# Convolution sums kept in two PSUM banks, with the weights' low parts and the running total made by GpSimd

## The chip, the cores and the metric

The kernel runs on one core of one Trainium2 chip. Its engines are TensorE (PE in the profile, with PEld for its weight loads), VectorE (DVE), ScalarE (ACT), GpSimd (POOL) and SyncE (SP, which here only issues DMAs). Each engine works through its own list of instructions in the order fixed when the program is built, and waits on semaphores for the others. The metric is the device time of one execution in microseconds, the median over runs. Before the change it is 1243.22 us (three runs, 1242.7 to 1243.86).

## The reference

One decoder layer on 1024 tokens of width 1024, float32. What matters here is the first half:

```
h = rmsnorm(x, norm_g) * (1 + scale) + shift
glu_a, glu_b, z_conv, q, k, v, z_att, g_conv, g_att = split(h @ w_in)
u = glu_a * sigmoid(glu_b)
u = causal depthwise convolution of u, 31 taps per channel, + conv_b
u = silu(layernorm(u, conv_ln_g, conv_ln_b))          # over the 1024 channels
y_conv = (u * silu(z_conv)) @ w_conv_out
... dilated attention of q, k, v gives y_att ...
merged = sigmoid(g_conv) * y_conv + sigmoid(g_att) * y_att
x = x + gate * (merged @ w_o);  out = rmsnorm(x, final_g)
```

The layer norm needs, for each token, the sum of the convolution's output over all channels, and then the sum of its squares.

## The kernel before

Channels lie on the 128 partitions and the 1024 tokens along the free dimension, so 1024 channels are eight tiles of 128 x 1024. To keep float32 precision at the speed of the matrix engine's fp32r type, every operand is split into a high part (rounded to fp32r, by ACT) and a low part (the rest, a subtraction). A product is then three matmuls: high by high, high by low, low by high (`mm3`, lines 72 to 75). `split` (line 55) makes both parts: line 57 is the ACT copy, line 58 the subtraction, on VectorE unless `lo_eng` names another engine.

An opening stage (to line 400) normalises x, makes the split input `hh`, `hl`, and computes the first projections. It uses a pool `pd` of eight PSUM banks of 128 x 512 float32. Its last matmuls are the first three projections (six banks called `first`) and, behind them, a row product (line 362) that ACT copies out at line 399.

The phase that the change touches is the loop at line 614 over the list `todo`. A `Unit` multiplies one column tile of 128 of `w_in` with the whole of h: two halves of 512 tokens, each 24 matmuls into one PSUM bank, which its `consume` then reads. A `Values` entry computes one group of the attention's v: eight tiles of 24 matmuls. `prepare` makes the split weights of the next entry while the present one runs: it loads a raw tile (three buffers, SP's queue) and splits it (two buffers each for high and low). For each of the eight channel tiles a `Glu` has two units: `sig` takes the sigmoid of `glu_b` on ACT (line 524), `glu` multiplies it with `glu_a` on VectorE (line 531) into a tile `u` of which there are two, whose 30 leading zeros GpSimd writes (line 529).

As soon as a `u` is complete, `conv` (line 437) is put into the list `behind`. It is a generator that issues the 31 taps on VectorE one at a time. Even taps are summed in `v` and odd taps in `v2`, so that neighbouring instructions do not depend on each other. The two are added (line 448), and `v` is added to the running total `tot1` over the channel tiles (lines 451, 454). A pump decides how these instructions are strewn among the matmuls: each quarter of a unit (12 matmuls) gives a credit of `PIECE` = 2.75, each tap takes `OP` = 1.25 of it, and other work on VectorE takes its share by `spend`. The build then orders each engine's instructions by this order of issue and by when they are ready.

When `todo` reaches entry `last_tap` (27), all taps left are issued (`drain`), and `norm` (line 567) takes their place in `behind`: the mean from a matmul of `ones` with `tot1` (line 572), its subtraction (578), squares on ACT and their total `tot2` (585), a matmul for the column sums (line 125), the reciprocal root, its row (line 140), scaling (597), gating (601) and the split of the result for the output projection, which begins at line 664. At line 680 `pd_ctx` is closed and the attention opens its own PSUM pools.

All PSUM pools are opened with `reuse_waits="tile"`: a tile of a new pool waits for the old tiles that lay in its place, not for the whole old pool. In the program before, other PSUM pools give their first tile their first bank.

Of the kernel before, what the change touches and what calls it, by code (L numbers as in the profile page):

```python
# [8 lines left out]
F32 = mybir.dt.float32  # L9
# [7 lines left out]
P = 128  # L17
S = 1024
D = 1024
KT = 8  # L20
TAPS = 31
# [18 lines left out]
def layer(ctx: ExitStack, tc: tile.TileContext, a, out):  # L40
    nc = tc.nc
    ctx.enter_context(nc.allow_non_contiguous_dma(reason="small gathers of row maxima"))
    add, mult, sub, mx = ALU.add, ALU.mult, ALU.subtract, ALU.max
# [5 lines left out]
    def psum_pool(name, **kw):  # L49
        return tc.tile_pool(name=name, space=PSUM, reuse_waits="tile", **kw)  # L50
# [4 lines left out]
    def split(hi, lo, raw, lo_eng=None):  # L55

        nc.scalar.activation(hi, raw, AF.Copy)  # L57
        (lo_eng or nc.vector).tensor_sub(lo, raw, hi.bitcast(F32))  # L58

    def load_raw(src, n=1024):  # L60
        raw = wpool.tile([P, n], F32, name="wraw", tag="wraw", bufs=3)
        nc.sync.dma_start(raw, src)
        return raw

    def weights(src, n=1024, lo_eng=None):
        raw = load_raw(src, n)
        hi = wpool.tile([P, n], F32R, name="whi", tag="whi")
        lo = wpool.tile([P, n], F32R, name="wlo", tag="wlo")
        split(hi, lo, raw, lo_eng)
        return hi, lo  # L70
# [20 lines left out]
    cw = taps.tile([P, KT, TAPS], F32, name="cw")  # L91
    cvec = taps.tile([P, 3, KT], F32, name="cvec")
# [23 lines left out]
    pd_ctx = ExitStack()  # L116
    pd = pd_ctx.enter_context(psum_pool("pd", bufs=8))
# [53 lines left out]
    with sbuf_pool("start") as st, tc.manual_schedule(  # L171
# [117 lines left out]
        for n, (x, c) in enumerate(zip((spread, cb[:, halves[1]]), halves)):  # L289
            nc.vector.tensor_tensor_reduce(out=wa_t[KT][:, c], in0=x, in1=wa_t[KT][:, c], scale=1.0, scalar=0.0,  # L290
                                           op0=mult, op1=add, accum_out=(gcol if n == 0 else scol)[:, 0:1])
# [115 lines left out]
    def slot(tag, name, dt=F32, bufs=1):  # L407
        return pb.tile([P, S], dt, name=name, tag=tag, bufs=bufs)

    def temp(name):  # L410
        return slot("tmp", name, bufs=3)
# [3 lines left out]
    PIECE, OP, HALF = 2.75, 1.25, 0.7  # L415
# [3 lines left out]
    def spend(us):  # L419
        credit[0] -= us  # L420

    def pump(us):
        credit[0] = min(credit[0] + us, 2 * PIECE)
        while credit[0] > 0 and behind:
            try:
                spend(next(behind[0]))
            except StopIteration:
                behind.pop(0)

    def drain():  # L430
        while behind:
            pump(2 * PIECE)

    tot1 = slot("l0", "tot1")
    v_t = [None] * KT

    def conv(ct, u):
        v = v_t[ct] = slot(f"v{ct}", f"v{ct}")
        v2 = temp("v2")
        nc.vector.tensor_scalar(v, u[:, 0:S], cw[:, ct, 0:1], cvec[:, 0, ct:ct + 1], op0=mult, op1=add)  # L440
        yield HALF
        nc.vector.tensor_scalar(v2, u[:, 1:1 + S], cw[:, ct, 1:2], None, op0=mult)
        yield HALF
        for k in range(2, TAPS):
            d = v2 if k % 2 else v
            nc.vector.scalar_tensor_tensor(d, u[:, k:k + S], cw[:, ct, k:k + 1], d, op0=mult, op1=add)  # L446
            yield OP
        nc.vector.tensor_add(v, v, v2)
        yield OP
        if ct == 0:  # L450
            nc.vector.tensor_copy(tot1, v)
            yield HALF
        else:
            nc.vector.tensor_add(tot1, tot1, v)
            yield OP

    def wide(half):
        return slice(half * 512, half * 512 + 512)

    class Unit:  # L460
# [3 lines left out]
            self.u, self.consume, self.cost = u, consume, cost  # L464

        def prepare(self):
            spend(OP)
            self.w = weights(a["w_t"][self.u])

        def run(self):  # L470
            hi, lo = self.w
# [12 lines left out]
    class Values:  # L484
# [5 lines left out]
        def prepare(self):  # L490
            self.w = []
            for kp in range(4):
                raw = load_raw(a["w_v"][self.g, kp])
                hi, lo = slot(f"z{kp}", f"vh{kp}", F32R), slot(f"z{4 + kp}", f"vl{kp}", F32R)
                split(hi, lo, raw)
                spend(OP)
                self.w.append((hi, lo))

        def run(self):
# [15 lines left out]
    class Glu:  # L515
# [10 lines left out]
        def glu(self, half, s, ps):  # L526
            if not half:
                self.u = up.tile([P, TAPS - 1 + S], F32, name="u", tag="u", bufs=2)
                nc.gpsimd.memset(self.u[:, 0:TAPS - 1], 0.0)
            o = TAPS - 1 + half * 512  # L530
            nc.vector.tensor_mul(self.u[:, o:o + 512], ps, self.sb[:, s])
            if half:
                behind.append(conv(self.ct, self.u))
# [33 lines left out]
    def norm():  # L567
        mean = up.tile([P, TAPS - 1 + S], F32, name="mean", tag="u", bufs=2)[:, 0:S]
        for half in range(2):
            s = wide(half)  # L570
            pm = bank()
            nc.tensor.matmul(pm, ones, tot1[:, s], start=True, stop=True)
            nc.scalar.activation(mean[:, s], pm, AF.Copy, scale=1.0 / D)
        yield 2 * PIECE
        lrow = up.tile([P, TAPS - 1 + S], F32, name="lrow", tag="u", bufs=2)[:, 0:S]
        tot2 = slot("l0", "tot2")
        for ct in range(KT):
            nc.vector.tensor_sub(v_t[ct], v_t[ct], mean)
            yield OP
            if ct == 0:  # L580
                nc.scalar.activation(tot2, v_t[ct], AF.Square)
            else:
                sq = temp("sq2")
                nc.scalar.activation(sq, v_t[ct], AF.Square)
                nc.vector.tensor_add(tot2, tot2, sq)
                yield OP
        yield PIECE
        pc = bank()[:, 0:8]
        col_sums(pc, tot2)
        lcols = rstd_cols(pc, "l")  # L590
        yield PIECE
        for half in range(2):
            half_row(lrow, lcols, half)
        yield PIECE
        for ct in range(KT):
            v = v_t[ct]
            nc.vector.tensor_mul(v, v, lrow)
            yield OP
            sg_ = temp("sgu")
            nc.scalar.activation(sg_, v, AF.Silu, scale=cvec[:, 1, ct:ct + 1], bias=cvec[:, 2, ct:ct + 1])  # L600
            nc.vector.tensor_mul(v, sg_, sz_t[ct])
            yield OP
            hi = slot(f"z{ct}", f"uh{ct}", F32R)
            lo = slot(f"v{ct - 1}" if ct else "l0", f"ul{ct}", F32R)
            split(hi, lo, v)
            yield OP
            ch[ct], cl[ct] = hi, lo
# [3 lines left out]
    for f, bb in ((g_.sig, first[0:2]), (g_.glu, first[2:4]), (second.sig, first[4:6])):  # L611
        for half in range(2):
            f(half, wide(half), bb[half])
    for n, unit in enumerate(todo):
        if n + 1 < len(todo):
            todo[n + 1].prepare()
        if n == last_tap:
            drain()
            behind.append(norm())
        for _ in unit.run():  # L620
            pump(PIECE)
# [65 lines left out]
    pd = c_ctx.enter_context(psum_pool("pd2", bufs=2))  # L687
# [140 lines left out]
    def pieces():  # L828

        for u in range(units):  # L830
            (hi, lo), consume = made_w.pop(u)
            for half in range(2):
                s = slice(half * 512, half * 512 + 512)
                ps = bank()
                for k in range(KT):
                    c = slice(k * P, (k + 1) * P)
                    mm3(ps, hi[:, c], lo[:, c], hh[:, k, s], hl[:, k, s], k == 0, k == KT - 1)
                    if k == 3:
                        yield None, (raw_for, u + 2) if half else (prepare, u + 1)
                yield lambda half=half, s=s, ps=ps: consume(half, s, ps), None  # L840

    k2, q2, v2 = {}, {}, {}
# [283 lines left out]
    for x, it in ((101, att_again(0)), (102, att_again(1)), (105, att_again(2)), (106, w_out(0, 0)), (109, w_out(0, 1)),  # L1126
                  (110, w_out(0, 2)), (111, first_ao())):
        in_steps(it, [x, x + 2])
    raw_for(0)
    prepare(0)  # L1130
    stream = pieces()

# [64 lines left out]
    pd = ctx.enter_context(psum_pool("pd3", bufs=8))  # L1197
# [12 lines left out]
    for d in range(KT):  # L1210
# [6 lines left out]
        hi, lo = hh[:, d, :], hl[:, d, :]  # L1217
# [127 lines left out]
```

## Time and profile before

| | |
|---|---|
| median of three runs | 1243.22 us |
| the profiled execution, first to last instruction | 1241.9 us |
| its granted TensorE clock, mean | 0.998 |
| PE busy | 1230.6 us, 6234 matmuls |
| VectorE busy | 909.5 us, 1500 instructions |
| ScalarE busy | 511.8 us, 1026 instructions |
| GpSimd busy | 91.1 us, 79 instructions |

The profile shows one execution; its time is the span from the first to the last instruction, and no other time of that execution is given. Groups of instructions are shown as: line, engine, operation, output tile <- input tiles, shapes, count, then total busy time in us and the mean of one in ns, then the engine's idle time just before them and what ended it. A timeline row has the start in us, the length in us, then the instruction; rows next to each other that are alike are merged with their count, and the length then covers all of them. A row of waits reads: who waited, for whom, the total in us, how often, the longest. Lengths of matmuls overlap, so the step from start to start tells PE's pace.

### The profile page before, as it was taken

What the parts mean: (1) busy time and instruction counts of PE and PEld (TensorE: products, weight loads), DVE (VectorE), ACT (ScalarE), POOL (GpSimd) and SP (SyncE); (2) the same over time, 40 slices, a digit from 0 to 9 for tenths busy, and PEclk for the clock granted to TensorE, in tenths of its full rate; (3) what the DMA queues carried; (4) which work ended last, traced back from release to release, by engine and by line L of the source; (5) the groups of instructions that cost most, each with busy time, mean ns of one, the idle gap of its engine ahead of it and who ended that gap; (6) DMA issues with size and microseconds to landing.
All of it is one profiled execution on the core that took longest, in us unless ns stands there. A gap on an engine that the chain in (4) does not pass through costs nothing.

```text
span 1241.9 us, 17026 instructions
## 1 busy us (share of the span) xinstructions
PE 1230.6 (99%) x6234; PEld 1033.2 (83%) x6234; DVE 909.5 (73%) x1500; ACT 511.8 (41%) x1026; POOL 91.1 (7%) x79
## 2 busy tenths in 40 slices
PE   9999999999999999999999999999999999999997
PEld 7787888888888888888888888888888888888886
DVE  7867999999999986873435657777786762449454
ACT  5653112111222235930114666666666665345211
POOL 0000000000000000000031111111111012100000
PEclk9999999999999999999999999999999999999999
DMA  9532311311211112355636555575666574668231
GB/s 358 195 106 72 114 52 50 110 60 51 86 54 49 51 55 80 127 172 203 191 74 165 128 139 145 157 186 145 161 187 151 138 183 130 207 232 297 87 102 68
DMA packets 89896, 165.09 MB, mean 133 GB/s; under 512 B 28563, under 2 KB 42195, under 8 KB 89814
## 3 DMA queue, kind: packets, MB, share of 16 engines
q1 hardware_dynamic: 73136, 157.40, 42.6%
q10 hardware_dynamic: 16678, 6.61, 2.0%
q8 instruction: 49, 0.80, 0.3%
q14 instruction: 33, 0.27, 0.1%
HBM read 105.48 MB, written 27.04 MB: 107 GB/s over the span
## 4 chain that ended last, share of the span: by engine, by line
PE 92%; DMA 3%; DVE 3%; ACT 1%; issue 1%; DVEq 0%; ACTq 0%; SPq 0%
PE d L73 22%; PE d L75 22%; PE d L74 22%; PE o L957 4%; PE s L920 3%; PE t L936 3%; PE d L1250 2%; PE d L1248 2%; PE d L506 2%; PE d L1249 2%; PE d L507 2%; PE d L505 2%; DMA sgr<-ascr 1%; DMA x<-in_xT 1%; PE d L271 1%
## 5 line engine op out<-in xcount | busy, mean ns | idle before, releaser
L73 PE MATMUL d<-hh,whi 128*128 128x512 f32 x1072 | 419.9, 392 | 0.0
L75 PE MATMUL d<-hh,wlo 128*128 128x512 f32 x1072 | 417.9, 390 | 0.0
L74 PE MATMUL d<-hl,whi 128*128 128x512 f32 x1072 | 417.9, 390 | 0.0
L446 DVE SCALAR_TENSOR_TENSOR v<-u,cw,v 128x1024 f32<-128x1024 f32 x232 | 280.3, 1275 | 0.0
L75 PEld LDWEIGHTS d<-hh,wlo 128*128 128x128 f32 x1072 | 201.3, 188 | 42.7
L73 PEld LDWEIGHTS d<-hh,whi 128*128 128x128 f32 x1072 | 201.4, 188 | 39.1 <-issue 0.2
L74 PEld LDWEIGHTS d<-hl,whi 128*128 128x128 f32 x1072 | 201.4, 188 | 38.7 <-issue 0.2
L57 ACT ACTIVATE whi<-wraw 128x512 fp32r<-128x512 f32 (+1 forms) x104 | 83.9, 827 | 212.3 <-PE d L74 203.1
L58 POOL TENSOR_TENSOR wlo<-wraw,whi 128x512 fp32r<-128x512 f32 (+1 forms) x56 | 81.7, 1476 | 636.0 <-ACT whi L57 624.2
L925 DVE CUSTOM_DVE_ANT_0 sb<-s,mask 128x128 f32<-128x128 f32 (+1 forms) x192 | 59.7, 348 | 53.6 <-PE s L920 52.3
L929 ACT ACTIVATE sb<-sb,stats 128x128 f32<-128x128 f32 (+1 forms) x192 | 84.8, 443 | 30.5 <-DVE stats L925 30.2
L936 PE MATMUL t<-ident,sb 128*128 128x128 f32 x280 | 73.7, 276 | 0.1
L957 PE MATMUL o<-ph,vt 128*64 128x128 f32 (+1 forms) x432 | 65.9, 253 | 0.0
L58 DVE TENSOR_TENSOR wlo<-wraw,whi 128x1024 fp32r<-128x1024 f32 (+1 forms) x48 | 54.8, 1141 | 14.6 <-ACT whi L57 14.1
L751 ACT ACTIVATE ph<-t 128x384 fp32r<-128x384 f32 (+2 forms) x96 | 45.8, 477 | 36.8 <-PE t L936 28.4
L754 DVE TENSOR_TENSOR pl<-t,ph 128x384 fp32r<-128x384 f32 (+2 forms) x96 | 52.0, 541 | 10.0 <-ACT ph L751 9.4
L920 PE MATMUL s<-k,ql 128*128 128x128 f32 (+1 forms) x192 | 55.0, 292 | 0.0
L957 PE MATMUL o<-pl,vt 128*64 128x128 f32 (+1 forms) x216 | 52.8, 261 | 0.0
L672 DVE TENSOR_TENSOR gs<-d,sgc 128x512 f32<-128x512 f32 x16 | 11.1, 691 | 54.9 <-PE d L75 48.6
L1250 PE MATMUL d<-oh,hl 128*128 128x512 f32 (+1 forms) x136 | 51.2, 376 | 0.0
L1248 PE MATMUL d<-oh,hh 128*128 128x512 f32 (+1 forms) x136 | 51.2, 376 | 0.0
L920 PE MATMUL s<-k,q 128*128 128x128 f32 (+1 forms) x192 | 51.1, 272 | 0.0
(242 smaller groups left out, 1917.0 us busy)
## 6 DMA issues: line engine op xcount, KB each, us to landing
wraw<-in_w_t SPq DMA_DIRECT2D x67, 512.0 KB, 4.2
k<-kqp SPq DMA_DIRECT2D x96, 128.0 KB, 2.3
q<-kqp SPq DMA_DIRECT2D x96, 128.0 KB, 2.4
wa<-in_w_ada SPq DMA_DIRECT2D x16, 512.0 KB, 6.1
ql<-kqp SPq DMA_DIRECT2D x48, 128.0 KB, 2.4
wg<-wscr SPq DMA_DIRECT2D x48, 128.0 KB, 3.1
wraw<-in_w_v SPq DMA_DIRECT2D x11, 512.0 KB, 3.6
vscr<-gs SPq DMA_DIRECT2D x16, 256.0 KB, 2.0
```

The source lines that it names most:

```text
L57: nc.scalar.activation(hi, raw, AF.Copy)
L58: (lo_eng or nc.vector).tensor_sub(lo, raw, hi.bitcast(F32))
L73: nc.tensor.matmul(ps, lh, rh, start=start, stop=False)
L74: nc.tensor.matmul(ps, lh, rl, start=False, stop=False)
L75: nc.tensor.matmul(ps, ll, rh, start=False, stop=stop)
L446: nc.vector.scalar_tensor_tensor(d, u[:, k:k + S], cw[:, ct, k:k + 1], d, op0=mult, op1=add)
L920: products.append((w, lambda c=c, w=w, l=x[:, ts_], r=k[:, ks], i=i: nc.tensor.matmul(ps[:, c:c + w], l, r, start=i == 0, stop=i == 1)))
L929: nc.scalar.activation(sb[:, c:c + w], sb[:, c:c + w], AF.Exp, bias=stats[:, t, h, 1:2], scale=-1.0, accum_out=stats[:, t, h, 0:1])
L936: yield from ((lambda c=c: nc.tensor.transpose(ps[:, c:c + P], sb[:, c:c + P], ident)) for c in range(0, o, P))
L957: nc.tensor.matmul(out_, l, r, **kw))
L1248: nc.tensor.matmul(ps, hh[:, k, c], rh, start=k == 0, stop=False)
L1250: nc.tensor.matmul(ps, hl[:, k, c], rh, start=False, stop=k == KT - 1)
```

## The change

The convolution has one chain in place of two, summed in a PSUM tile `acc` of 128 x 1024 float32 (two banks, one buffer); the last tap writes `v` in SBUF. The running total goes to GpSimd. The low parts of the weights of all units in this phase and of the `Values` go to GpSimd, and with them the `spend(OP)` that stood for them. After the six `first` banks have been handed to their readers, the pool of eight banks is closed, and a pool of six and the pool for `acc` are opened.

```diff
     def conv(ct, u):
         v = v_t[ct] = slot(f"v{ct}", f"v{ct}")
-        v2 = temp("v2")
-        nc.vector.tensor_scalar(v, u[:, 0:S], cw[:, ct, 0:1], cvec[:, 0, ct:ct + 1], op0=mult, op1=add)
-        yield HALF
-        nc.vector.tensor_scalar(v2, u[:, 1:1 + S], cw[:, ct, 1:2], None, op0=mult)
-        yield HALF
-        for k in range(2, TAPS):
-            d = v2 if k % 2 else v
-            nc.vector.scalar_tensor_tensor(d, u[:, k:k + S], cw[:, ct, k:k + 1], d, op0=mult, op1=add)
+        acc = pconv.tile([P, S], F32, name="acc", tag="acc")
+        nc.vector.tensor_scalar(acc, u[:, 0:S], cw[:, ct, 0:1], cvec[:, 0, ct:ct + 1], op0=mult, op1=add)
+        yield OP
+        for k in range(1, TAPS):
+            nc.vector.scalar_tensor_tensor(v if k == TAPS - 1 else acc, u[:, k:k + S], cw[:, ct, k:k + 1], acc,
+                                           op0=mult, op1=add)
             yield OP
-        nc.vector.tensor_add(v, v, v2)
-        yield OP
         if ct == 0:
-            nc.vector.tensor_copy(tot1, v)
-            yield HALF
+            nc.gpsimd.tensor_copy(tot1, v)
         else:
-            nc.vector.tensor_add(tot1, tot1, v)
-            yield OP
+            nc.gpsimd.tensor_add(tot1, tot1, v)
...
         def prepare(self):
-            spend(OP)
-            self.w = weights(a["w_t"][self.u])
+            self.w = weights(a["w_t"][self.u], lo_eng=nc.gpsimd)
...
-                split(hi, lo, raw)
-                spend(OP)
+                split(hi, lo, raw, nc.gpsimd)
                 self.w.append((hi, lo))
...
             f(half, wide(half), bb[half])
+    pd_ctx.close()
+    pd = pd_ctx.enter_context(psum_pool("pd1", bufs=6))
+    pconv = pd_ctx.enter_context(psum_pool("pconv", bufs=1))
     for n, unit in enumerate(todo):
```

## The prediction

> **What bounds the kernel now.** I read the busy times first, then who waited for whom on the matrix engine (PE), then the busy time by stretch for the convolution phase, and last single matmuls of that phase.
>
> ```profile
> PE 1230.6 (99%) x6234; PEld 1033.2 (83%) x6234; DVE 909.5 (73%) x1500; ACT 511.8 (41%) x1026; POOL 91.1 (7%) x79
> ```
>
> A busy PE is not yet a PE at its peak, since matmuls overlap in the record. So the next two views ask whether it waits, and whether it starts matmuls at an even pace.
>
> ```profile
> PE d L140 <- ACT rrow L141: 1.3, 1, 1.3
> PE d L257 <- POOL ones L86: 1.1, 1, 1.1
> PE d L271 <- ACT hh L235: 0.8, 1, 0.8
> PE d L75 <- DVE wlo L58: 0.3, 1, 0.3
> ```
>
> ```profile
> 102.00:455.00 353.00, 353.00 (x1559) 292.31 (x1558) 351.89 (x310) 67.97 (x87) 4.02 (x6) 1.00 0.21 66
> 455.00:547.00 92.00, 92.00 (x416) 75.83 (x415) 71.00 (x71) 61.53 (x67) 0.00 (x0) 1.00 0.35 112
> ```
>
> ```profile
> 411.12 0.39 PE L74 MATMUL d<-hl,whi 128*128 128x512 f32 x1
> 411.35 0.39 PE L75 MATMUL d<-hh,wlo 128*128 128x512 f32 x1
> 411.57 0.39 PE L73 MATMUL d<-hh,whi 128*128 128x512 f32 x1
> ```
>
> The four waits are all that PE has, 3.5 us in the whole program. L140, L257 and L271 belong to the opening stage; in L75 the weights' low part is late by 0.3 us, once. In the stretches the columns are length, then PE, PEld, DVE, ACT, POOL, each with its count, then the granted clock. From 102 to 455 us (the taps) PE is busy 353.00 of 353.00, with the clock at 1.00. 353 / 1559 is 0.226 us for a matmul, which is also the step between the quoted starts (0.23, 0.22). No matmul in this phase comes late. DVE is as full (351.89), but it finishes in time. The change takes work from DVE; PE's 1559 matmuls stay, at the same clock. So I look for what could make PE wait, not for what DVE saves.
>
> **The change, part by part.** These are the rows for what is removed, added and moved.
>
> ```profile
> L446 DVE SCALAR_TENSOR_TENSOR v<-u,cw,v 128x1024 f32<-128x1024 f32 x232 | 280.3, 1275 | 0.0
> L440 DVE TENSOR_SCALAR v<-u,cw,cvec 128x1024 f32<-128x1024 f32 x8 | 6.4, 804 | 0.0
> L531 DVE TENSOR_TENSOR u<-d,sigb 128x512 f32<-128x512 f32 x16 | 10.6, 683 | 7.2 <-ACT sigb L524 5.8 <-PE d L75 1.4
> L58 DVE TENSOR_TENSOR wlo<-wraw,whi 128x1024 fp32r<-128x1024 f32 x41 | 50.0, 1220 | 11.1 <-ACT whi L57 10.5
> L58 POOL TENSOR_TENSOR wlo<-wraw,whi 128x1024 fp32r<-128x1024 f32 x8 | 19.9, 2482 | 91.7 <-ACT whi L57 79.8 <-PE d L75 11.8
> L529 POOL MEMSET u<- 128x30 f32 x8 | 4.2, 534 | 360.4 <-DVE v L446 279.2 <-DVE hl L383 81.3
> ```
>
> *One chain in place of two.* A channel tile now takes one tensor_scalar and 30 scalar_tensor_tensor (29 before), all on one accumulator in PSUM, each reading what the one ahead of it wrote. Gone from DVE are the second tensor_scalar, the sum of the two chains (L448) and the running total (L454). Before, neighbours worked on v and v2 in turn and overlapped. What dependence costs shows where the trace has it:
>
> ```profile
> 408.10 1.27 DVE L446 SCALAR_TENSOR_TENSOR v<-u,cw,v 128x1024 f32<-128x1024 f32 x1
> 409.30 0.80 DVE L440 TENSOR_SCALAR v<-u,cw,cvec 128x1024 f32<-128x1024 f32 x1
> 410.02 1.21 DVE L448 TENSOR_TENSOR v<-v,v 128x1024 f32<-128x1024 f32 x1
> 411.15 0.74 DVE L442 TENSOR_SCALAR v<-u,cw 128x1024 f32<-128x1024 f32 x1
> 411.82 1.22 DVE L454 TENSOR_TENSOR tot<-tot,v 128x1024 f32<-128x1024 f32 x1
> 412.95 1.22 DVE L58 TENSOR_TENSOR wlo<-wraw,whi 128x1024 fp32r<-128x1024 f32 x1
> ...
> 452.35 1.23 DVE L448 TENSOR_TENSOR v<-v,v 128x1024 f32<-128x1024 f32 x1
> 453.60 1.22 DVE L454 TENSOR_TENSOR tot<-tot,v 128x1024 f32<-128x1024 f32 x1
> ```
>
> From 408.10 to 409.30 the next instruction starts 1.20 us after a tap of 1.27 us: an overlap of 0.07. At 452.35 to 453.60 the second needs the first's result, and the step is 1.25 for 1.23: no overlap, 0.02 more. A dependent tap is therefore 1.275 + 0.02 to 0.03, say 1.30 us, against 1.20.
>
> No row shows DVE writing PSUM. The nearest rows read it:
>
> ```profile
> L1252 DVE TENSOR_TENSOR y<-y,xt 128x512 f32<-128x512 f32 x15 | 10.4, 692 | 0.5
> L1251 DVE TENSOR_TENSOR y<-d,gate_b 128x512 f32<-128x512 f32 x15 | 10.3, 690 | 28.2 <-PE d L1250 28.2
> ```
>
> One operand from PSUM costs 690 ns against 692 with both in SBUF, so reading PSUM costs nothing. For writing I take nothing too, with bounds from -0.10 (the overlap comes back: 1.20) to +0.15 us a tap (twice the overlap lost above; an estimate). The tensor_scalar into PSUM lies between its 0.80 and a tap's 1.275; I take 1.28.
>
> DVE's sum for 102 to 455 us: 8 x (1.28 + 30 x 1.30) + 16 glu halves x 0.683 = 322.2 + 10.9 = 333 us, against 351.9 now; the low parts are gone from it. Some 20 us of the 353 come free, and PE was not waiting for them: worth 0. That cover fails once a tap exceeds (353 - 10.9 - 10.2) / 240 = 1.38 us.
>
> [...]
>
> *Low parts and total on POOL.* In the same stretch 25 low parts of units, 8 of the value weights and 8 totals take 41 x 2.48 = 102 us of POOL's 353: load enough is free. What counts is the lead. The high part is made as the unit before starts:
>
> ```profile
> 411.54 1.06 ACT L57 ACTIVATE whi<-wraw 128x1024 fp32r<-128x1024 f32 x1 [4.61 <-PE d L74]
> ```
>
> It ends at 412.60, POOL's low part at 415.1. The unit that wants it begins 48 matmuls x 0.226 = 10.9 us after about 411.6, at 422.5: 7.4 us to spare, where DVE (412.95 + 1.22) left 8.3. The raw buffer goes back to the load queue 0.9 us later, out of a unit's 10.9 and with three buffers. Worth 0. The cover is gone if something ahead of the low part holds POOL. In POOL's order now stand the total, which waits for a conv's last tap, and the memset of u (0.53 us, waits for the conv two before), and low parts queue behind both.
>
> *DVE and POOL side by side.* Two rows show what a low part on POOL does to DVE:
>
> ```profile
> 1074.12 2.78 DVE L1038 TENSOR_TENSOR wg<-wg 128x512 f32<-128x512 f32 x1
> ...
> 1073.31 3.05 POOL L58 TENSOR_TENSOR wlo<-wraw,whi 128x1024 fp32r<-128x1024 f32 x1 [8.93 <-ACT whi L57]
> ```
>
> An instruction with two SBUF operands took 2.78 us beside it, about 2.09 over the 0.69 of its kind (row L1252). In the change taps have one of theirs in PSUM, as glu has, so I charge nothing there. The layer norm (455 to 547) is full of two-operand instructions; six low parts at 2.09, less 1.22 each that DVE no longer spends, add at most 5.2 us. DVE is busy 71.00 of those 92 us, so this fits.
>
> PE meets DVE there in the sums of squares:
>
> ```profile
> 457.81 1.88 PE L572 MATMUL d<-tot,ones 128*128 128x512 f32 x4
> 484.06 1.84 PE L125 MATMUL d<-ones,tot 128*128 128x1 f32 x16
> ...
> 475.13 3.87 DVE L585 TENSOR_TENSOR tot<-tot,sq 128x1024 f32<-128x1024 f32 x3
> ```
>
> L125 stands 5.1 us behind its input (479.0). Without `spend(OP)` in `prepare`, the pump reaches it (15 steps of 1.25 and a pause of 2.75 are 21.5 credits) one quarter unit sooner: 22.0 after quarter 1 of the third unit, where it was 22.25 after quarter 2. So it moves 12 x 0.226 = 2.7 us forward, and 2.4 us stay. Contention of one low part (+0.9 net) fits, of two as well. Worth 0, at most +1. The mean (L572) wants the total, ready at 454.8 now and earlier after: 0.
>
> *Six banks.* A half takes 24 x 0.226 = 5.4 us, so a bank has 5 x 5.4 = 27 us to be read in; ACT, busy 68 of 353 us, reads soon, and glu waits its turn on DVE. Worth 0 while DVE keeps up. At the switch of pools it is not:
>
> ```profile
> 96.25 0.59 ACT L399 ACTIVATE vs<-d 2x512 f32<-2x512 f32 x1 [4.20 <-PE d L362]
> 98.45 2.07 ACT L524 ACTIVATE sigb<-d 128x512 f32<-128x512 f32 x4
> ...
> 95.83 0.39 PE L362 MATMUL d<-wl,s_parts 128*2 128x512 f32 x1
> 96.05 0.39 PE L73 MATMUL d<-hh,whi 128*128 128x512 f32 x1
> ```
>
> Now the first unit begins at 96.05, straight behind the row product, in a bank read long ago. A new pool starts with its own first bank; in the program before, other PSUM pools give their first tile their first bank, and bank 0 holds the row product here. ACT has read it at 96.84. So PE waits 0.8 us; bounds 0 (a bank that is free) and 4.5 (a bank read last, at 100.52).
>
> **Sum.** 1241.9 + 0.8 + 0 = 1242.7 us of span. The median of the runs, 1243.22, lies 1.3 above the profiled span of 1241.9; so **1244.0** is forecast. About 0.2%, 2.5 us, is what a measurement of this kernel can tell from no change; the forecast is inside that.
>
> **The rivals.**
>
> *Slower: the PSUM chain makes DVE the bound.* Above 1.38 us a tap DVE needs more than the stretch, PE waits for glu and for the total at L572, and every 0.01 us costs 240 x 0.01 = 2.4 us: 1.40 gives 1249, 1.45 (the upper bound) 1261. For it: dependence on every tap, and writes to PSUM that no row shows. Against: 0.08 us of margin, and 690 against 692 ns.
>
> *Slower: POOL's queue.* The order is fixed at compile time. If real taps run later than it was laid out for, the total waits at POOL's head and the next low part is late. Of the 7.4 us the total's own 2.48 comes off, and about 5 us of DVE lag is free. An error of 0.04 us a tap would pile up 240 x 0.04 = 9.6 us, some 4 to 5 of it for PE: 1248 to 1249. For it: DVE has only 20 us of slack to catch up in. Against: now, after 300 us of taps, the order still fits: the low part starts 0.35 us after its high part (412.60 to 412.95).
>
> *Slower: the pool switch costs the full 4.5 us*, if the first bank is one that ACT reads last, or the new pool waits for all of the old one: 1247.7.
>
> *Faster.* PE has 0.3 us of waits outside the opening, none in this phase. More than 0.2% can't come from there: 1243 at best, whatever DVE gains.
>
> **How the numbers follow.** The forecast 0.67; the DVE bound 0.11, POOL's queue 0.10, the switch 0.08; 0.04 for something faster that I don't see. Slower by over 0.2% is 0.11 + 0.10 + 0.08, rounded up for norm's wait: 0.30; same 0.66; faster 0.04. The range runs from 1242.3 (nothing lost, the runs' scatter) to 1253: it takes in the switch, POOL's queue and the lower end of the DVE bound.
>
> **What would show it.** Right: PE without waits from 102 to 547 us, but for under a microsecond at the first unit; DVE about 333 of 353 us busy there, taps 1.30 us apart; POOL about 105; low parts ending 7 us ahead of their unit. Wrong: taps over 1.38 apart; PE waiting for POOL's wlo, or for DVE's u at a bank; L125 or L572 preceded by a gap; four microseconds at 96. A clear gain would refute the reading that PE alone sets this phase.

## The result and the profile after

The changed kernel takes 1250.78 us (median of four runs, 1248.96 to 1252.95) against 1243.37 us for the kernel before beside it (1242.7 to 1243.86). The ratio is 1.006, with a 95% interval of 1.0046 to 1.0075: slower by 7.4 us. The profiled execution took 1248.96 us, the fastest of the four, and spans 1247.2 us, 5.3 more than before. So the time lies in the range that was given, but not where the likeliest case put it.

Busy times of the changed kernel, from the first part of its page:

```profile
PE 1231.5 (99%) x6234; PEld 1032.8 (83%) x6234; DVE 885.8 (71%) x1443; ACT 518.4 (42%) x1031; POOL 208.9 (17%) x128
```

VectorE has 24 us less to do, GpSimd 118 us more, and ScalarE has five instructions more. They are table loads, which in this trace stand where ScalarE goes over from one function to another: 29 where there were 24, 1.28 us each.

Who PE waited for in the changed kernel (total in us, times, longest):

```profile
PE d L75 <- POOL wlo L58: 3.3, 3, 1.6
PE d L140 <- ACT rrow L141: 1.2, 1, 1.2
PE d L257 <- POOL ones L86: 1.1, 1, 1.1
PE d L271 <- ACT hh L235: 0.9, 1, 0.9
PE d L73 <- ACT vs L399: 0.7, 1, 0.7
PE d L73 <- ACT whi L57: 0.6, 1, 0.6
```

The rows of L140, L257 and L271 are those of before. New are three waits for a low part from GpSimd, one for a high part from ScalarE, and the one at the switch of the pools (L399). The stretches of the changed kernel (length, then PE, PEld, DVE, ACT, POOL, clock):

```profile
102.00:455.00 353.00, 351.94 (x1553) 291.08 (x1552) 326.28 (x261) 67.60 (x87) 94.52 (x46) 1.00 0.21 66
455.00:547.00 92.00, 89.14 (x399) 72.49 (x398) 65.29 (x57) 63.33 (x67) 21.75 (x7) 1.00 0.32 103
```

The long stretch of the taps loses a single microsecond, the layer norm about three. The single matmuls show where. From the timeline of PE in the changed kernel:

```profile
95.83 0.39 PE L362 MATMUL d<-wl,s_parts 128*2 128x512 f32 x1
96.90 0.50 PE L73 MATMUL d<-hh,whi 128*128 128x512 f32 x1 [0.68 <-ACT vs L399]
...
119.03 0.39 PE L74 MATMUL d<-hl,whi 128*128 128x512 f32 x1
120.48 0.50 PE L75 MATMUL d<-hh,wlo 128*128 128x512 f32 x1 [1.06 <-POOL wlo L58]
120.81 0.39 PE L73 MATMUL d<-hh,whi 128*128 128x512 f32 x1
...
516.58 0.39 PE L74 MATMUL d<-hl,whi 128*128 128x512 f32 x1
517.66 0.50 PE L75 MATMUL d<-hh,wlo 128*128 128x512 f32 x1 [0.70 <-POOL wlo L58]
...
528.00 0.39 PE L75 MATMUL d<-hh,wlo 128*128 128x512 f32 x1
528.97 0.50 PE L73 MATMUL d<-hh,whi 128*128 128x512 f32 x1 [0.58 <-ACT whi L57]
...
529.54 0.40 PE L73 MATMUL d<-hh,whi 128*128 128x512 f32 x1
531.52 0.50 PE L75 MATMUL d<-hh,wlo 128*128 128x512 f32 x1 [1.58 <-POOL wlo L58]
```

The reading goes by steps from start to start, of which the usual one is 0.227 us. The five long ones are 1.07, 1.45, 1.08, 0.97 and 1.98 us (before the last a matmul's record is missing, so two usual steps come off). What is over is 0.84 + 1.22 + 0.85 + 0.74 + 1.53, and the matmul behind each gap takes 0.11 more as well (120.48 to 120.81 is 0.33): 5.7 us in all. The difference of the spans is 5.3. In the kernel before no step between 52 and 700 us is longer than 0.32 us, but for the mean's own few matmuls at 459, which both kernels have.

So the loss is at three places: the switch at 97 us (0.95), the third unit at 120 us (1.3), and three times in the norm at 517 to 532 us (3.5). None of them lies in the 300 us between, where the low parts on GpSimd come in time. The lists of ScalarE show what is late. First the changed kernel between the switch and the third unit:

```profile
100.39 1.08 ACT L57 ACTIVATE vh<-wraw 128x1024 fp32r<-128x1024 f32 x1
107.35 1.06 ACT L57 ACTIVATE vh<-wraw 128x1024 fp32r<-128x1024 f32 x1 [5.88 <-DMA wraw<-in_w_v]
114.55 1.06 ACT L57 ACTIVATE vh<-wraw 128x1024 fp32r<-128x1024 f32 x1 [6.14 <-DMA wraw<-in_w_v]
115.52 1.04 ACT L57 ACTIVATE whi<-wraw 128x1024 fp32r<-128x1024 f32 x1
```

The same of the kernel before:

```profile
100.38 1.08 ACT L57 ACTIVATE vh<-wraw 128x1024 fp32r<-128x1024 f32 x1
106.91 1.06 ACT L57 ACTIVATE whi<-wraw 128x1024 fp32r<-128x1024 f32 x1 [5.44 <-PE d L74]
```

`vh` is the high part of the value weights, `whi` that of the third unit. Before, `whi` came second, at 106.91. Now the list that the build lays out has two more `vh` ahead of it. Each waits about 6 us for its load, and `whi` comes at 115.52, for a unit that begins at 118.81. Then GpSimd's queue adds its part. Its timeline in the changed kernel:

```profile
115.69 2.40 POOL L58 TENSOR_TENSOR vl<-wraw,vh 128x1024 fp32r<-128x1024 f32 x1 [4.80 <-ACT vh L57]
118.06 2.37 POOL L58 TENSOR_TENSOR wlo<-wraw,whi 128x1024 fp32r<-128x1024 f32 x1
...
515.13 2.48 POOL L58 TENSOR_TENSOR wlo<-wraw,whi 128x1024 fp32r<-128x1024 f32 x1 [14.59 <-ACT whi L57]
528.99 2.47 POOL L58 TENSOR_TENSOR wlo<-wraw,whi 128x1024 fp32r<-128x1024 f32 x1 [11.38 <-ACT whi L57]
```

The third unit's low part stands behind a `vl` and ends at 120.43; PE starts with it at 120.48. The place in the queue matters: begun as soon as its high part was done (116.56), the low part would have ended near 119.0, ahead of the 119.26 at which PE's next matmul was due (an estimate from these rows). So this gap needs both, the late `whi` and the `vl` ahead of it on GpSimd. In the norm GpSimd is free and had been waiting 14.59 and 11.38 us for the high part. There it is ScalarE alone that is late, and GpSimd's 2.48 us come on top of that.

### The profile page after: what moved, and what is told of

It reads as the page before. It is cut to its first block, busy times and chain, and to the rows that moved or that the text cites. A ratio compares the mean times of both kernels' runs of the same rounds, so it can differ in the third digit from the quotient of the medians.

```text
span 1247.2 us, 17047 instructions
## 1 busy us (share of the span) xinstructions
PE 1231.5 (99%) x6234; PEld 1032.8 (83%) x6234; DVE 885.8 (71%) x1443; ACT 518.4 (42%) x1031; POOL 208.9 (17%) x128
## 4 chain that ended last, share of the span: by engine, by line
PE 92%; DMA 2%; DVE 2%; issue 1%; ACT 1%; POOL 1%; SPq 0%; DVEq 0%; ACTq 0%; POOLq 0%
PE d L73 23%; PE d L75 22%; PE d L74 22%; PE o L952 4%; PE s L915 3%; PE t L931 3%; PE d L1244 2%; PE d L1243 2%; PE d L498 2%; PE d L1245 2%; PE d L499 2%; PE d L497 2%; DMA wraw<-in_w_v 1%; DMA x<-in_xT 1%; PE d L271 1%
## 5 line engine op out<-in xcount | busy, mean ns | idle before, releaser
L75 PE MATMUL d<-hh,wlo 128*128 128x512 f32 x1072 | 418.2, 390 | 3.3 <-POOL wlo L58 3.3
L443 DVE SCALAR_TENSOR_TENSOR acc<-u,cw,acc 128x1024 f32<-128x1024 f32 x232 | 299.1, 1289 | 7.7
L58 POOL TENSOR_TENSOR wlo<-wraw,whi 128x512 fp32r<-128x512 f32 (+1 forms) x89 | 166.3, 1879 | 758.4 <-ACT whi L57 758.4
L75 PEld LDWEIGHTS d<-hh,wlo 128*128 128x128 f32 x1072 | 201.2, 188 | 47.3 <-POOL wlo L58 4.6
L952 PEld LDWEIGHTS o<-ph,vt 128*64 128x64 f32 x432 | 48.3, 136 | 2.4
L497 PE MATMUL d<-vh,hh 128*128 128x512 f32 x128 | 49.8, 389 | 0.0
```

What stands on the lines that cost most here:

```text
L75: nc.tensor.matmul(ps, ll, rh, start=False, stop=stop)
L443: nc.vector.scalar_tensor_tensor(v if k == TAPS - 1 else acc, u[:, k:k + S], cw[:, ct, k:k + 1], acc, op0=mult, op1=add)
L952: nc.tensor.matmul(out_, l, r, **kw))
```

## Experiments

Two theories stood against each other. By the first, the loss is order: ScalarE's high parts stand later in its list, because the change took `spend(OP)` out and let the value weights through sooner. By the second, it is GpSimd itself: its queue, or its quarrel with VectorE over SBUF. Eleven kernels were run in three groups, each group beside its own runs of the kernel before (medians 1244.68, 1243.45 and 1244.14 us). The ratios stand in the record with their intervals and are not exactly the quotients of the medians (for `all_three`, 1.0011 where the medians give 1.0021).

**The changed kernel once more** (`again`).

> The changed kernel once more, as the yardstick for the other runs on this chip. In its profiled execution PE lost 1.0 us at the switch of pools, 1.3 us at a unit near 120 us and 3.5 us at three places between 517 and 532 us, 5.7 us together, while the medians differ by 7.4. Expected: 1249 to 1253 us, gaps at the same three places, and a spread between runs of some 4 us, since the order of instructions is fixed and only the meeting of DVE and POOL differs.

1251.08 us, ratio 1.0065 (1.0052 to 1.0078), span 1248.5. The long steps are at the same five matmuls, so the gaps belong to the program and are no accident of one execution.

**Credit back in the norm** (`norm_spend`), the low parts staying on GpSimd:

```diff
         def prepare(self):
+            if self in todo[last_tap + 1:]:
+                spend(OP)
             self.w = weights(a["w_t"][self.u], lo_eng=nc.gpsimd)
```

> Only one thing is put back: while the layer norm runs (units prepared after the last tap), prepare spends OP from the pump's credit again. Low parts stay on POOL. Theory A (order): the 3.5 us between 517 and 532 us come from the pump, which without that spend issues the norm's steps sooner, so that ACT's list alternates between sigmoid and silu and loads its table five times more (29 loads against 24), and the weights' high parts stand too late in it. Then this run loses these gaps although POOL and DVE meet as before: 1245 to 1248 us. Theory B (contention): DVE's two-operand steps, held up by the low parts on POOL, make ACT and the high parts late; then nothing is won: 1249 to 1253.

**The same with these low parts on VectorE** (`norm_dve`):

```diff
+            late = self in todo[last_tap + 1:]
+            if late:
+                spend(OP)
-            self.w = weights(a["w_t"][self.u], lo_eng=nc.gpsimd)
+            self.w = weights(a["w_t"][self.u], lo_eng=None if late else nc.gpsimd)
```

> In the layer norm the spend is put back and the low parts of those units go back to DVE; all else stays as changed. Theory A (order): the same as with the spend alone, 1245 to 1248 us. Theory B (contention): only this run, not the one with the spend alone, loses the gaps between 517 and 532 us: 1245 to 1248 against 1249 to 1253. If both act, this run is faster than the one with the spend alone by what the meeting of POOL and DVE costs, 1 to 2 us, and its runs lie closer together.

The ratios are 1.0021 (1.0011 to 1.0031) and 1.0026 (1.0014 to 1.0037), 1247.12 and 1247.79 us: the same. PE's waits in `norm_spend`:

```profile
PE d L75 <- DVE wlo L58: 1.7, 1, 1.7
...
PE d L75 <- POOL wlo L58: 1.1, 1, 1.1
...
PE d L73 <- ACT vs L399: 0.7, 1, 0.7
```

The only wait for GpSimd that is left is that of the third unit, and the one for `whi` is gone. In both kernels no long step is left in the norm. With the credit in place, which engine subtracts makes no difference there. The credit moves the norm's pieces back by a quarter unit: from the mean's first matmul to that of L125 it is 26.24 us in `norm_spend` (460.23 to 486.47), 23.53 in the changed kernel (460.16 to 483.69) and 26.25 in the kernel before. And the high parts come forward among these pieces. The same `whi` on ScalarE in the changed kernel, and then in `norm_spend`:

```profile
514.01 1.04 ACT L57 ACTIVATE whi<-wraw 128x1024 fp32r<-128x1024 f32 x1
```

```profile
511.88 1.05 ACT L57 ACTIVATE whi<-wraw 128x1024 fp32r<-128x1024 f32 x1
```

It is 2.1 us earlier, and the gap at 517.66 was 0.85. Low parts on VectorE without the credit were not run. By the rows, one of 1.22 us on VectorE in place of 2.48 on GpSimd would end 1.26 us sooner, which is more than the gap of 0.85 and most of that of 1.53 (an estimate, if VectorE is free). So the slower engine may have a share in the loss that these runs do not separate. The wait of 1.7 us for VectorE's `wlo` lies in the output stage late in the program; the kernel before has one of 0.3 there, and it comes and goes between runs.

**The value weights' low parts back on VectorE** (`values_dve`):

```diff
-                split(hi, lo, raw, nc.gpsimd)
+                split(hi, lo, raw)
+                spend(OP)
```

> The low parts of the value weights go back to DVE with their spend; all else stays as changed. Theory: POOL makes these low parts as soon as it can, which frees the raw buffers early and lets the value weights' loads go ahead of the third unit's, so that this unit's high part is made at 115.5 us (106.9 before the change) and PE waits 1.3 us for its low part at 120 us. Then this gap goes: 1.3 us off the changed kernel, about 1249.5, with DVE still far from full (326 of 353 us, and 9 more). Rival: the low part is late because it queues on POOL behind a value low part (115.69 to 118.09 us); the gap goes as well, but the third unit's high part stays where it was, at 115.5.

1249.97 us, ratio 1.005 (1.0038 to 1.0063). The 1.1 us less than in `again` lie within the intervals, so it is the trace that decides. ScalarE's list has one `vh` fewer ahead of `whi`:

```profile
106.96 1.06 ACT L57 ACTIVATE vh<-wraw 128x1024 fp32r<-128x1024 f32 x1 [5.23 <-DMA wraw<-in_w_v]
108.22 1.06 ACT L57 ACTIVATE whi<-wraw 128x1024 fp32r<-128x1024 f32 x1 [0.20 <-PE d L74]
```

The third unit's high part comes 7.3 us earlier and the gap at 120 us is gone, while those at the switch and in the norm stay. Had it been GpSimd's queue alone, `whi` would have stayed at 115.5. The `vl` is gone from that queue as well, so the run does not part the two.

**The row product earlier** (`row_early`), to take the wait at the switch away: its 16 matmuls are issued before the last group of the projections, so that ScalarE could copy it out while they run.

```diff
+            if kt == 7:
+                p_row = bank()[0:2]
+                shift_row(p_row, slice(0, KT))
             for i, (wh, wl) in enumerate(u_w):
...
-            if kt == 7:
-                p_row = bank()[0:2]
-                shift_row(p_row, slice(0, KT))
```

> The changed kernel with the opening stage's row product (16 matmuls) issued ahead of the last 18 matmuls of the first projections instead of behind them, so that ACT has read its bank long before the new pool's first tile takes it. Theory: PE's gap at the switch of pools (0.84 us, and 0.11 behind it) goes and nothing else changes: 1.0 us off the changed kernel, some 1250. Rival: the new pool waits for other tiles of the old one too; then a gap stays at 97 us, up to the 4.5 us that the last of ACT's sigmoids would cost.

A miss, and a dear one: 1257.11 us, ratio 1.0096 (1.0079 to 1.0114). ScalarE's copy does not move:

```profile
96.38 0.59 ACT L399 ACTIVATE vs<-d 2x512 f32<-2x512 f32 x1 [0.52 <-PE d L75]
```

It waits for PE's last L75, a matmul that has nothing to do with the row. The copy's target `b_row` has the tag `vs` with one buffer, and so had `u2l`, the low weights that PE reads to the end. And the rest moves back: the third unit's `whi` comes at 118.12, 2.6 us later than in the changed kernel. PE waits for it longer, and then runs slowly for a while:

```profile
119.56 0.40 PE L74 MATMUL d<-hl,whi 128*128 128x512 f32 x1
123.04 0.55 PE L75 MATMUL d<-hh,wlo 128*128 128x512 f32 x1 [3.08 <-POOL wlo L58]
123.39 0.63 PE L73 MATMUL d<-hh,whi 128*128 128x512 f32 x1
123.82 0.63 PE L74 MATMUL d<-hl,whi 128*128 128x512 f32 x1
...
126.38 0.58 PE L74 MATMUL d<-hl,whi 128*128 128x512 f32 x1
```

The step is 0.43 us in place of 0.227 (123.39 to 123.82). From 123.39 to 126.38 there are seven such steps, 1.4 us over the usual. The mean granted clock of this execution is 0.995, of the changed kernel's 0.998.

**The three edits together** (`all_three`: `norm_dve`, `values_dve` and `row_early`).

> All three repairs at once: the norm's units with low parts on DVE and their spend, the value weights' low parts on DVE with their spend, and the row product ahead of the last projections. The PSUM chain, the total and the other units' low parts on POOL stay. If the three gaps (1.0, 1.3 and 3.5 us) are all that the change costs, PE has no gap from 52 to 700 us and the time is that of the kernel before within 0.2%. It can't be faster by more than the scatter, since PE had nothing to win in this phase. If something else costs time as well, 1 to 2 us remain.

1246.01 us, ratio 1.0011 (1.0002 to 1.002). The long step at the switch is the only one left between 52 and 700 us, apart from the mean's own at 459. None was expected; `row_early` shows why this one stays.

**And the row's copy in another place** (`row_free`):

```diff
-        b_row = st.tile([P, S], F32, name="vs", tag="vs", bufs=1)[0:2, 0:512]
+        b_row = st.tile([P, D], F32, name="wa", tag="wa", bufs=4)[0:2, 0:512]
```

> The three edits of all_three with one more: the copy of the row product goes into a tile of the tag "wa", which nothing on PE is still reading, in place of the tag "vs", whose one buffer is the low weight tile of PE's last matmuls ahead of the switch. If that shared place is what held ACT's copy, and through it PE's first matmul in the new pool, the step of 1.06 us near 97 us goes and PE has no step over 0.25 us from 52 to 700 us; span within 0.5 us of the kernel before, ratio 1.000 (0.999 to 1.001). Rival: the switch itself holds PE (all banks of the old pool, or the semaphore's way from ACT to PE): the step stays at 0.7 to 1.1 us, ratio about 1.001, as all_three.

1244.34 us, ratio 1.0003 (0.9994 to 1.0011): the time of before. PE's timeline at the switch:

```profile
95.81 0.39 PE L75 MATMUL d<-hh,u2l 128*128 128x512 f32 x1
96.04 0.39 PE L73 MATMUL d<-hh,whi 128*128 128x512 f32 x1
96.27 0.39 PE L74 MATMUL d<-hl,whi 128*128 128x512 f32 x1
96.88 0.50 PE L75 MATMUL d<-hh,wlo 128*128 128x512 f32 x1 [0.23 <-POOL wlo L58]
```

The step into the new pool is 0.23 us, so the pool switch itself costs nothing. Not all went as expected: a shorter gap of 0.4 us is left two matmuls later, where the first unit's low part is just late on GpSimd. The stretch of the taps is full again in this kernel:

```profile
102.00:455.00 353.00, 353.00 (x1559) 292.40 (x1558) 333.81 (x268) 68.50 (x88) 76.56 (x38) 1.00 0.21 66
```

VectorE has 19 us of the 353 free here, and the time is that of the kernel before: what VectorE saves is worth nothing.

**The credit back everywhere** (`spend_all`), all low parts on GpSimd: `spend(OP)` again in `Unit.prepare` and behind each `split` of `Values`. Its build has 29 table loads, as the changed kernel's has.

> The changed kernel with spend(OP) back in the preparation of every unit and of the values, while all low parts stay on GpSimd. The built list of ACT still has the value weights' three high parts ahead of the third unit's, and 29 table loads. Theory, that what counts is the list that comes out of the build, not the credit itself: gaps of PE near 97, 120, 518 and 530 us as in the changed kernel, 1249 to 1253 us, ratio 1.004 to 1.008. Rival, that the credit itself (PE's L125 standing 2.7 us later) is what helped in norm_spend: no gaps in the norm, 1246 to 1248 us, ratio 1.002 to 1.003.

1247.29 us, ratio 1.0029 (1.0019 to 1.0039). My theory expected 1249 or more, so this was a miss, and it corrects the theory. The gap of the third unit stays (a step of 1.55 us at 120.49). The norm's gaps are gone but for one of 0.5 us at 539, with the same 29 table loads. GpSimd's timeline in `spend_all`:

```profile
510.13 3.54 POOL L58 TENSOR_TENSOR wlo<-wraw,whi 128x1024 fp32r<-128x1024 f32 x1 [12.87 <-ACT whi L57]
524.85 2.49 POOL L58 TENSOR_TENSOR wlo<-wraw,whi 128x1024 fp32r<-128x1024 f32 x1 [11.18 <-ACT whi L57]
```

The same two low parts start 5.0 and 4.1 us earlier than in the changed kernel. So the five table loads more are not by themselves the loss. What counts is where the high part stands among ScalarE's work, and the two places have separate causes: in the norm the credit that was taken out, at the third unit the engine that makes the value weights' low parts (with the credit alone the gap stays, with the low parts on VectorE and the credit it goes; VectorE without the credit was not run).

**Each half of the change by itself.** `pool_alone` is the kernel before with only the low parts and the total on GpSimd (two chains in SBUF, eight banks); `chain_alone` is the kernel before with only the PSUM chain and the six banks (low parts, credits and total as before).

> The kernel before with one half of the change: low parts and total on POOL, but the taps as before, two chains in SBUF with eight banks. Each tap now has two operands in SBUF. If POOL holds such an instruction up for as long as the one seen (about 2.1 us more), 41 POOL instructions of the phase add 86 us to DVE's 352 - 50 = 302 us: 388 us against the 353 there are, so DVE becomes the bound: 1265 to 1290 us, with PE waiting for glu. If a tap is not held up, it is the kernel before with DVE at 302 of 353 us: 1243 to 1250.

> The other half alone: one chain in PSUM, six banks, but low parts, their spends and the total on DVE. Taps 1.33 us apart, as in the changed kernel's trace: 8 x (1.35 + 30 x 1.33) + 10.9 for glu + 33 low parts x 1.22 + 8 totals x 1.2 = 391 us of DVE work against the 353 there are, so PE waits for some 30 to 40 us: 1270 to 1285. If PE could do without what DVE owes at the end (the layer norm's slack takes it), the loss is smaller, 1250 to 1260.

1315.26 us, ratio 1.0559 (1.0536 to 1.0582), and 1269.65 us, ratio 1.0202 (1.0186 to 1.0218). Alone, the halves cost 72 and 26 us; together 7. `pool_alone` lies 25 us above the range expected of it, `chain_alone` just below its own. The groups of `pool_alone` (count, total busy in us, mean in ns):

```profile
L446 DVE SCALAR_TENSOR_TENSOR v<-u,cw,v 128x1024 f32<-128x1024 f32 x232 | 342.1, 1544 | 0.0
L58 POOL TENSOR_TENSOR wlo<-wraw,whi 128x1024 fp32r<-128x1024 f32 x41 | 134.0, 3273 | 324.9 <-ACT whi L57 324.9
```

A tap with both operands in SBUF went from 1275 to 1544 ns beside GpSimd's work, and the low part from 2482 to 3273. 232 x 0.27 = 62 us more on an engine that had one to spare, against some 50 saved: VectorE is busy 352.96 of the 353 us, and PE waits 45.5 us for low parts and 7.5 for high ones, not for `glu` as expected. In `chain_alone` the new wait, but for the 0.7 us at the switch, is at one place:

```profile
PE d L568 <- DVE tot L450: 21.7, 1, 21.7
```

The mean waits for the total. From the changed kernel's 326 us of VectorE, 33 low parts and 8 totals of 1.22 us make 376, which is 23 over the 353, or some 30 with the small gaps between dependent taps. The total is ready at 483.58 us, 28.8 later than in the kernel before (454.82). Behind that wait PE runs slowly for a while: the mean's four matmuls take 3.78 us, where they took 1.88, and the usual step is back from 487.96. The mean granted clock from 455 to 547 us, the wait included, is 0.87, in the changed kernel 1.00.

**Two accumulators in PSUM** (`two_accs`), to find what a tap's 1.33 us is made of: even taps go to `acc`, odd ones to `acc2`, a sum at the end, four banks for the units.

```diff
+        acc2 = pconv.tile([P, S], F32, name="acc2", tag="acc2")
...
+            d = acc2 if k % 2 else acc
+            nc.vector.scalar_tensor_tensor(v if k == TAPS - 1 else d, u[:, k:k + S], cw[:, ct, k:k + 1], d, op0=mult, op1=add)
```

> The changed kernel with two PSUM accumulators used in turn (even taps, odd taps), their sum at the end, and four banks in place of six for the units. If the 1.33 us from tap to tap comes of dependence, steps fall back to 1.20 to 1.22 us; if it is the price of PSUM for each instruction, they stay at 1.29 to 1.33. For the time it does not matter by the theory that the order of ACT's list makes the loss: the gaps of PE near 97, 120, 518 and 530 us stay, 1249 to 1253 us. Rival, that DVE's slower tap has a part in the loss: with steps of 1.21 us the gaps shrink and the time comes to 1246 or less.

VectorE's timeline in the changed kernel, and then in `two_accs` (merged rows: five and four taps):

```profile
101.86 6.59 DVE L443 SCALAR_TENSOR_TENSOR acc<-u,cw,acc 128x1024 f32<-128x1024 f32 x5
```

```profile
103.76 4.86 DVE L447 SCALAR_TENSOR_TENSOR acc<-u,cw,acc 128x1024 f32<-128x1024 f32 x4
```

Less the last tap's own length (the groups' means are 1289 and 1281 ns), four steps take 5.30 us and three take 3.58: 1.325 us a step in one chain, 1.193 in two. In the kernel before the step was 1.20 in SBUF. So the price is dependence, 0.13 us a tap, and for a tap PSUM adds nothing that shows (1281 ns against 1275 in SBUF). A chain's first instruction is another matter: the tensor_scalar took 1347 ns into PSUM (changed kernel) against 804 into SBUF, eight times in the program. For the time it does not matter: 1251.05 us, ratio 1.0056 (1.0043 to 1.0069), with the five gaps where they were.

## Why the prediction came out as it did

**What held.** PE sets this phase, and VectorE's savings are worth nothing. `row_free` is the test: VectorE 19 us emptier, the time of before. The cover has an edge too: `chain_alone`, with more work on VectorE, goes over it and waits 21.7 us. The dependent tap was taken as 1.30 us and measured 1.325, inside the bounds and below the 1.38 at which the cover fails; VectorE's 333 us came out as 326 busy and some 9 of small gaps between dependent taps. Only the tensor_scalar lies outside its bounds (1.35 us where 1.28 was taken), half a microsecond in all. The switch was put at 0.8 us, for ScalarE's copy of the row product, and cost 0.95 behind that copy; by `row_early` and `row_free`, both the row product's place in the order and the copy's place in SBUF held it. The total at GpSimd's head, the mean and the six banks cost nothing, as said.

**What failed.** By the prediction's own signs its mechanism failed: PE waits for POOL's `wlo`, three times. That 1250.78 us lies inside the range is in part luck, since the range reached that far for POOL's queue behind a late total and for a VectorE over its cover, and neither came about. The first step that failed is "Worth 0" for the low parts on GpSimd. Its lead of 7.4 us was read from one unit at 411 us, deep in the steady stretch, and taken for all. It holds there, but not where the phase begins and ends. At the third unit the low part ends 1.2 us after PE's matmul was due. The rival "POOL's queue" looked at the right danger, a low part too late, but for the total ahead of it on GpSimd. What was late is its input, the high part on ScalarE, and at the third unit it then stood behind a value weight's low part.

The second failed step is "one quarter sooner", which gave the removed `spend(OP)` "worth 0, at most +1". I followed one matmul, L125, and asked whether its input was ready. That much was right: it comes 2.7 us sooner behind the mean, and its input is ready 1.3 us ahead of it (482.43 and 483.69). But the credit also sets where the units' high parts fall among the norm's pieces on ScalarE. That is worth 3.5 us by the steps, and 4.0 us by the medians of `again` and `norm_spend` (1251.08 and 1247.12).

The third is that `Values` entered only as load on GpSimd (8 low parts in the 102 us): with its low parts there its high parts move up on ScalarE, for 1.3 us at the third unit. Why the build places them so was not tried; it may be that their buffers come free in time sooner.

The contention in the norm was rightly put at 0 to +1: with the credit back, the time is the same with the low parts on either engine (1247.12 and 1247.79 us).

**What stays open.** The gaps explain the 5.3 us between the profiled spans, not all of the 7.4 between the medians. The profiled execution is the fastest of its four, and they spread over 4.0 us where the four of the kernel before beside them spread over 1.2; but in the larger groups that came later the kernel before spreads over 2.7 to 4.2. In `row_early` PE ran at half its pace behind such a gap (0.43 us a step for 0.227); if some executions of the changed kernel do that behind one or two of theirs, that would be the rest. In `values_dve` it looks that way: its two slowest runs (1251.67 and 1253.77 us) have a mean granted clock of 0.996 and 0.995, the other four 0.998 or more. But the four runs of the changed kernel all have 0.998, and the one trace of each of its two sets of runs shows no such pace, so this is not settled.

## What to carry to other kernels

When work moves to another engine, read its lead at the first and the last units of the phase as well as in the middle, and follow its input back: here the producer that came late was a third engine, whose list the build had laid out anew. In a kernel whose order comes from credits, a credit that is removed is an edit to every engine's order, and can cost more than the work it stood for. Take the two halves of a change apart before judging them: these two cost 72 and 26 us alone, and nearly nothing together in `row_free`, where the order was mended and some of the low parts were back on VectorE.

## What the runs showed of the hardware

Where a tap has its operands made a difference beside GpSimd's work. With `u` and `v` both in SBUF a tap took 1275 ns in the kernel before, where GpSimd was busy for 4.02 us of the 353, and 1544 in `pool_alone`, where it was busy for 119.87. With the accumulator in PSUM it took 1289 in the changed kernel (GpSimd busy for 94.52 us), and 1281 in two chains (95.23). It took 1289 in `chain_alone` too, where GpSimd was busy for only 0.74 us of the 353. That is why the two halves of this change belong together: GpSimd takes some 50 us off VectorE, without which the longer chain goes over the 353, and with the chain in PSUM a tap took no longer beside GpSimd than without it.

GpSimd's own instructions took longer in some places as well: the low part's mean was 3273 ns in `pool_alone`, 2482 in the kernel before. In the changed kernel's norm, where VectorE's sums have both operands in SBUF, one low part took 6.39 us on GpSimd, against 2.40 among the taps; the five behind it up to 547 us took 2.47 to 2.80:

```profile
472.30 6.39 POOL L58 TENSOR_TENSOR wlo<-wraw,whi 128x1024 fp32r<-128x1024 f32 x1 [11.32 <-ACT whi L57]
```

PE's half pace followed pauses of different lengths. In `row_early` it followed a step of 3.48 us, shown above, but also one of 1.98 us at 535.69, of the kind that the changed kernel has at 531.52 without it:

```profile
535.69 0.51 PE L75 MATMUL d<-hh,wlo 128*128 128x512 f32 x1 [1.58 <-POOL wlo L58]
...
537.04 0.63 PE L73 MATMUL d<-hh,whi 128*128 128x512 f32 x1
537.46 0.63 PE L74 MATMUL d<-hl,whi 128*128 128x512 f32 x1
```

The step is 0.42 us here (537.04 to 537.46), and the mean granted clock from 455 to 547 us is 0.98, in the changed kernel 1.00. The trace counts 3.08 of the 3.48 us as waiting, and 1.58 of the 1.98. The changed kernel's wait at 531.52 is 1.58 us too, and behind it the usual step is back after one matmul (531.86 to 532.09). So these runs show no length of pause that goes with the slow pace; why it followed here and not in the changed kernel is open.
